# Differential attention scores: two products over 128 rows per map, or three over 64 rows with the two maps one above the other in the array

## The chip, the cores and the metric

The kernel runs on one core of one Trainium2 chip. The metric is the device time of one execution in microseconds (us); 729.48 us is the median of three runs of the kernel before (729.27, 729.48 and 730.88).

## The reference, cut to what matters

The program is a two-layer sequence model for 512 tokens of width 1024: a Mamba-2 layer (projections, a causal convolution, a chunked state-space scan, an out projection), then a layer of differential attention with eight heads, then a last RMS norm. All is float32. The change concerns the scores of the attention:

```python
DIFF_HEADS, DIFF_HEAD_DIM = 8, 64
k = kv[..., :1024].reshape(b, s, DIFF_HEADS, 2, DIFF_HEAD_DIM)      # two key maps per head
q = qg[..., :1024].reshape(b, nblk, 128, DIFF_HEADS, 2, DIFF_HEAD_DIM)
...
scores = einsum("bhiqd,bhikd->bhiqk", qb, k) / sqrt(64)             # i: the two maps
scores = scores - slopes[h] * dist
probs = softmax(where(key chunk <= query chunk, scores, -inf))
weights = probs[:, :, 0] - lam * probs[:, :, 1]
out = einsum("bhqk,bhke->bqhe", weights, v)
```

Each head thus has two score maps, and each is a product over only 64 features.

## The kernel before, in words

**Precision.** Nearly every product is made of three. An operand is kept as a rounded high part of type float32r and a low part (the value less its high part, rounded to float32r too); high by high, high by low and low by high are summed in PSUM, low by low is left out. `mm3` issues these three for the projections. TensorE works through one float32r product in one pass.

**The two streams on TensorE.** In the second half of the program, from about 440 us on, one stream `stream_b` yields the dense products in the order of `ORDER_B`: projections `pv` (values), `pk`, `pq`, `pt` (keys, queries and gates, two of them out of one weight tile, in `feat_proj`) and `pb` and `pc` (the output projection). A loop over the eight heads h and the four query blocks t of 128 rows draws on it: `scores(h, t)`, a third of a share of dense work, the transposes of the block before (`turn`), the rest of the share, the products with the values of the block before (`values`). The dense work is there to cover what DVE and ACT do between the two steps of a block. `T.on` makes TensorE issue in just the order in which the code is written; DVE and ACT are reordered by the scheduler in this part, by its own model, except at the very end.

**Keys and queries.** `feat_proj` leaves the 128 features of one head (64 of map 0, then 64 of map 1) on the 128 partitions of a PSUM bank `pf` (`pk` and `pq` in the profile), all 512 tokens wide. Lines 750 to 758 take it apart by map m. For keys, slot m of the tile `k2` gets the map's high half in its own 64 partitions and its low half in the other 64: one ACT copy and one DVE subtraction of 64 x 512 for each map. For queries, slot m of `q2` gets the high half in both places (two ACT copies for each map), and the tile `q_lo` gets the low half in the map's own partitions; the other 64 partitions of `q_lo` are zero, set once by four memsets on GpSimd (line 897). All ACT and DVE rows of this have the line 55 of a helper; they go by their tiles `k`, `q` and `q_lo`.

**Scores.** `scores(h, t)` works on n = 128 (t + 1) keys. For each map it takes a PSUM bank `sc` and issues two products over all 128 partitions: `q2` by `k2` (high by high from the one half of the partitions, high by low from the other) and `q_lo` by `k2` (low by high, and zero by the rest). DVE then adds the distance penalty and takes the row maximum out of the bank (`s<-sc,bias` in the profile), ACT makes the exponential. There are 32 such visits with four products each, that is, 16 products of each of the widths 128, 256, 384 and 512 in each of the two kinds.

**PSUM.** `ss_bank` hands out banks in turn: three buffers under the tag `ss`, and each fourth one in this part from the four `mm` buffers of the dense stream.

**A product of half width in the first half.** `ssd` makes the scan's products `pyd` from 64 stationary columns each, for the two halves of the output partitions (line 615, `for r in (slice(0, 64), slice(64, 128))`): 16 such products for each bank, issued alternately for the one and the other half. They are of plain float32, which the trace shows as two records per product.

Of the kernel before, what the change touches and what calls it, by code (L numbers as in the profile page):

```python
# [9 lines left out]
F32 = mybir.dt.float32  # L10
F32R = mybir.dt.float32r
I32 = mybir.dt.int32
AF = mybir.ActivationFunctionType
ALU = mybir.AluOpType
# [3 lines left out]
P = 128  # L18
S = 512
# [44 lines left out]
def trunk(ctx, tc, x, x_t, par, w_dt, w_in, w_out, w_kvqg, w_bo, d_skip, lam_qk, fin_g, out):  # L64
    nc = tc.nc
    V, A, T = (Ordered(tc, e) for e in (nc.vector, nc.scalar, nc.tensor))
    GP = nc.gpsimd
# [7 lines left out]
    def mm_bank(name):  # L75
        return psum.tile([P, 512], F32, tag="mm", name=name, bufs=4)
# [4 lines left out]
    def ss_bank(name):  # L81
        turns[0] += 1
        tag = "mm" if turns[0] % turns[1] >= 3 else "ss"
        return psum.tile([P, 512], F32, tag=tag, name=name, bufs=3 if tag == "ss" else 4)

    def long_bank(name):
        return psum.tile([P, 512], F32, tag="long", name=name)
# [118 lines left out]
    def use_b(seg, first=None, pace=None):  # L206
        i = segs.index(seg)
        while pieces:
            lay(pieces.pop(0))
        if i + 2 < len(segs) and fetched[0] == i + 2:  # L210
            loaded[i + 2] = load(i + 2)
        if seg == ("o", 3, 0):
            for piece in loaded.pop(i + 2)():
                lay(piece)
        if i + 1 in loaded:
            new = loaded.pop(i + 1)()
            pace = pace or 32 // len(new)
            pieces.extend(p + (pace if k else first or pace,) for k, p in enumerate(new))
        return ready.pop(seg)
# [15 lines left out]
    def mm3(ps, lhs, rhs, first, last, **kw):  # L235
        (lh, ll), (rh, rl) = lhs, rhs
        T.matmul(ps, lhsT=lh, rhs=rh, start=first, stop=False, **kw)
        T.matmul(ps, lhsT=lh, rhs=rl, start=False, stop=False, **kw)
        T.matmul(ps, lhsT=ll, rhs=rh, start=False, stop=last, **kw)
# [191 lines left out]
    q2 = sm.tile([P, P], F32, name="q2")  # L431
# [281 lines left out]
    cp = ctx.enter_context(tc.tile_pool(name="cp", bufs=1))  # L713
# [12 lines left out]
                yield 1  # L726
            A.copy(v_sb[:, t, cs], pv[:, 0:256])

    q_lo = [cp.tile([P, 2, S], F32R, name=f"q_lo{i}") for i in range(2)]
    kT, qT, gT, oT = {}, {}, {}, {}  # L730

    def feat_proj(pair):
        wh, wl = use_b((pair[0], pair, 0))
        for i in range(2):
            kind, h = pair[2 * i], int(pair[2 * i + 1])
            pf = mm_bank(f"p{kind}{h}")
            cs = slice(i * P, (i + 1) * P)
            for k in range(KD):
                mm3(pf, (wh[:, k, cs], wl[:, k, cs]), (hh[:, k, :], hl[:, k, :]), k == 0, k == KD - 1)
                yield 2  # L740
            if kind == "t":

                th = small.tile([P, S], F32, tag="wide", name=f"th{h}", bufs=2)
                A.activation(th, pf, AF.Tanh, scale=0.5)
                gt = cp2.tile([P, S], F32, tag="gt", name=f"gt{h}", bufs=3)
                V.scalar_tensor_tensor(out=gt, in0=th, scalar=1.0, in1=pf, op0=ALU.add, op1=ALU.mult)
                gT[h] = gt
            else:

                two = cp2.tile([P, 2, S], F32R, tag=f"{kind}2", name=f"{kind}2_{h}", bufs=4 if kind == "k" else 2)  # L750
                for m in range(2):
                    own, far = slice(64 * m, 64 * m + 64), slice(64 - 64 * m, 128 - 64 * m)
                    A.copy(two[own, m, :], pf[own, :])
                    if kind == "q":
                        A.copy(two[far, m, :], pf[own, :])
                    V.tensor_tensor(out=two[far, m, :] if kind == "k" else q_lo[h % 2][own, m, :], in0=pf[own, :],
                                    in1=two[own, m, :].bitcast(F32), op=ALU.subtract)
                (kT if kind == "k" else qT)[h] = two
            done.add(f"{kind}{h}")

# [17 lines left out]
    def stream_b():  # L778
        for it in ORDER_B:
            if it[0] == "c":  # L780
                yield from rows()
                return
            yield from b_out(int(it[1])) if it[0] == "b" else v_proj(int(it[1])) if it[0] == "v" else feat_proj(it)
            done.add(it)
# [3 lines left out]
    def scores(h, t):  # L788

        if t == 0:  # L790
            bias = cp2.tile([P, S], F32, tag="bias", name=f"bias{h}")
            V.tensor_scalar(out=bias, in0=dist, scalar1=-(2.0 ** (2 - h)), scalar2=None, op0=ALU.mult)
            st[h] = (bias, small.tile([P, 2, NT], F32, tag="mx", name=f"mx{h}"),
                     small.tile([P, 2, NT], F32, tag="sums", name=f"sums{h}"), [],
                     small.tile([P, NT], F32, tag="ratio", name=f"ratio{h}"), long_bank(f"po{h}"), [],
                     cp2.tile([P, NT, P], F32, tag="on", name=f"on{h}", bufs=2),
                     small.tile([P, NT], F32, tag="o_ss", name=f"o_ss{h}"))
        bias, mx, sums, s = st[h][0:4]
        k2, q2, ql = kT[h], qT[h], q_lo[h % 2]
        n = (t + 1) * P  # L800
        tq = slice(t * P, (t + 1) * P)
        s.append([cp2.tile([P, S], F32, tag=f"s{i}", name=f"s{h}_{t}_{i}", bufs=2) for i in range(2)])
        for i in range(2):
            ps = ss_bank(f"sc{h}_{t}_{i}")
            T.matmul(ps[:, :n], lhsT=q2[:, i, tq], rhs=k2[:, i, :n], start=True, stop=False)
            T.matmul(ps[:, :n], lhsT=ql[:, i, tq], rhs=k2[:, i, :n], start=False, stop=True)
            so = s[t][i][:, :n]
            V.tensor_tensor_reduce(out=so, in0=ps[:, :n], in1=bias[:, S - n:], scale=-0.125, scalar=3e38,
                                   op0=ALU.add, op1=ALU.min, accum_out=mx[:, i, t:t + 1])
            A.activation(so, so, AF.Exp, scale=-1.0, bias=mx[:, i, t:t + 1], accum_out=sums[:, i, t:t + 1])  # L810
# [81 lines left out]
    V.tensor_copy(dist, disti)  # L892
    A.activation(dist, dist, AF.Abs)
    GP.memset(dist[0:64, S - 64:S], BIG)
    for i in range(2):
        for m in range(2):
            GP.memset(q_lo[i][64 - 64 * m:128 - 64 * m, m, :].bitcast(F32), 0.0)
    lq = cp2.tile([P, 4, 64], F32, tag="gt", name="lq", bufs=3)
    nc.sync.dma_start(lq.rearrange("p a d -> p (a d)"), lam_qk.rearrange("a d -> (a d)").partition_broadcast(P))
    lqv = lq.rearrange("p (a b) d -> p a b d", b=2)  # L900
# [38 lines left out]
    def half(t, n):  # L939
        hs = slice(n * 512, (n + 1) * 512)  # L940
        return x_tok[:, t, hs], fg[:, hs], ot[t][:, hs], out[t * P:(t + 1) * P, hs]
# [40 lines left out]
    for h in range(DH):  # L982
        for t in range(NT):
            share = (13.0, 15.3, 17.6, 19.35)[t]
            if (h, t) == (DH - 1, 2):
                break
            scores(h, t)
            beside(share / 3)
            if h > 1 and t == 0:
                gate_head(h - 2)  # L990
            if last:
                turn(*last)
            beside(share * 2 / 3)
            if last:
                values(*last)
                if t == 0:
                    norm_head(h - 1)
            last = h, t


    h = DH - 1
    turns[:] = [0, 1]
    fg = res.tile([P, D], F32, tag="hT_lo", name="fg")
    nc.sync.dma_start(fg[:], fin_g.partition_broadcast(P))
    scores(h, 2)
    beside(6)
    gate_head(h - 1)
# [3 lines left out]
    norm_head(h, 0, 2)  # L1011
    beside(7.6)
    scores(h, 3)
    ot += [cp2.tile([P, D], F32, tag="k2", name=f"ot{t}", bufs=4) for t in range(NT)]
    beside(2)
# [45 lines left out]
    y, f, o, dst = half(3, 0)  # L1061
# [71 lines left out]
```

## Time and profile before

| What | Value |
|---|---|
| Median of three runs | 729.48 us (729.27 to 730.88) |
| The profiled execution: time, span | 729.15 us, 727.0 us |
| TensorE (PE) busy | 713.5 us, 98% of the span |
| TensorE weight loads (PEld) busy | 593.1 us, 82% |
| VectorE (DVE) busy | 528.0 us, 73% |
| ScalarE (ACT) busy | 433.7 us, 60% |
| GpSimd (POOL) busy | 117.7 us, 16% |
| HBM traffic | 97 GB/s over the span |
| Chain that ended last, share by engine | PE 90%, DVE 7%, ACT 1%, issue 1% |

A row of the trace's timeline gives the start in us, the time in us, the engine, the line, the operation, the tiles written and read, for TensorE the part of the array that is used (rows by columns), the shape, and how many instructions in a row are merged. TensorE's products are pipelined: the recorded time of one contains its way through the array, so a run of equal products starts one every 0.23 us though each is recorded with 0.40 us. What a product costs TensorE is the distance from its start to that of the next (its pitch). The busy time of PE is a union of such records and hides gaps that are shorter than the overlap. "PEld" rows are the loads of the stationary operand, which run beside the products.

### The profile page before, as it was taken

The page shows a single profiled execution, that of the slowest core. Times are in us where ns is not written, and L with a number is a line of the kernel's source. Part 1 is how long each engine was busy: PE and PEld are TensorE (multiplying, and loading weights), DVE is VectorE, ACT ScalarE, POOL GpSimd, SP SyncE. Part 2 cuts the span into 40 slices and gives each one's busy share as a digit, 9 for nine tenths or more (in the row PEclk, how much of TensorE's full clock was granted, in tenths as well). Part 3 has the DMA queues.
Part 4 walks back from the last instruction along what each step waited for, and adds up shares of the span by engine and source line. Part 5 has one row for each costly group of instructions (what it writes and reads, how often), then busy time and mean ns, then how long its engine had stood idle before and what let it go on. Part 6 is the DMA issues. An engine that isn't in the chain of part 4 may idle for free.

```text
span 727.0 us, 10819 instructions
## 1 busy us (share of the span) xinstructions
PE 713.5 (98%) x3989; PEld 593.1 (82%) x3989; DVE 528.0 (73%) x1202; ACT 433.7 (60%) x965; POOL 117.7 (16%) x158
## 2 busy tenths in 40 slices
PE   9999999999999999999999999999999999999996
PEld 7787888888888888887788869888988898889874
DVE  4688964979479668569995846657667857785886
ACT  5948573654735527527534348667766756756566
POOL 0108241412315024150110101000000000000002
PEclk9999999999999999999999999999999999999999
DMA  8634313314133231231122310331221131122003
GB/s 302 233 131 162 116 59 117 117 58 175 58 117 116 95 137 60 91 142 59 59 70 105 116 59 9 117 115 59 94 82 58 59 117 59 59 90 85 29 1 115
DMA packets 12916, 70.86 MB, mean 97 GB/s; under 512 B 1728, under 2 KB 2496, under 8 KB 5312
## 3 DMA queue, kind: packets, MB, share of 16 engines
q1 hardware_dynamic: 12576, 69.90, 26.5%
q8 instruction: 31, 0.51, 0.3%
q10 hardware_dynamic: 288, 0.28, 0.1%
q14 instruction: 21, 0.17, 0.1%
HBM read 68.02 MB, written 2.16 MB: 97 GB/s over the span
## 4 chain that ended last, share of the span: by engine, by line
PE 90%; DVE 7%; ACT 1%; issue 1%; POOL 0%; ACTq 0%; DVEq 0%; POOLq 0%
PE pg L55 21%; PE po L55 14%; PE pz L55 12%; PE pt L55 7%; PE pv L55 6%; PE pq L55 6%; PE pk L55 6%; PE pb L55 3%; PE sc L55 3%; PE pyd L55 2%; PE pc L55 2%; DVE wlo L55 2%; DVE xc L55 2%; PE pyt L55 1%; PE pxt L55 1%; PE psA L55 1%
## 5 line engine op out<-in xcount | busy, mean ns | idle before, releaser
L55 DVE SCALAR_TENSOR_TENSOR wlo<-raw,prm,whi 128x512 fp32r<-128x512 f32 (+1 forms) x256 | 150.4, 633 | 52.7 <-ACT whi L55 51.3
L55 ACT ACTIVATE whi<-raw,prm 128x512 fp32r<-128x512 f32 (+1 forms) x256 | 136.8, 606 | 81.4 <-PE pg L55 30.1
L55 PE MATMUL pg<-a_hi,whi 128*128 128x512 f32 x256 | 103.3, 404 | 1.5 <-DVE y_c L55 1.5
L55 PE MATMUL pg<-a_hi,wlo 128*128 128x512 f32 x256 | 102.3, 402 | 0.0
L55 PE MATMUL pg<-a_lo,whi 128*128 128x512 f32 x256 | 102.3, 400 | 0.0
L55 DVE SCALAR_TENSOR_TENSOR xc<-pg,prc,xc 128x511 f32<-128x511 f32 (+2 forms) x96 | 69.6, 738 | 4.8 <-ACT xc L55 4.4
L55 PEld LDWEIGHTS pg<-a_hi,whi 128*128 128x128 f32 x256 | 48.1, 188 | 13.1 <-issue 1.9
L55 PEld LDWEIGHTS pg<-a_hi,wlo 128*128 128x128 f32 x256 | 48.1, 188 | 11.0
L55 PEld LDWEIGHTS pg<-a_lo,whi 128*128 128x128 f32 x256 | 48.1, 188 | 10.7
L55 PE MATMUL po<-whi,yh 128*128 128x512 f32 x128 | 51.4, 402 | 1.5 <-DVE xc L55 0.8
L55 PE MATMUL po<-wlo,yh 128*128 128x512 f32 x128 | 51.1, 399 | 0.0
L55 PE MATMUL po<-whi,yl 128*128 128x512 f32 x128 | 50.4, 398 | 0.0
L55 PE MATMUL pz<-wlo,a_hi 128*128 128x512 f32 x128 | 50.3, 399 | 0.0
L55 PE MATMUL pz<-whi,a_lo 128*128 128x512 f32 x128 | 49.8, 398 | 0.0
L55 PE MATMUL pz<-whi,a_hi 128*128 128x512 f32 x128 | 49.6, 401 | 0.0
L971 POOL TENSOR_TENSOR ot<-ot,fg 128x512 f32<-128x512 f32 x4 | 5.1, 1289 | 256.9 <-ACT ot L55 256.9
L55 ACT ACTIVATE s<-s,mx 128x128 f32<-128x128 f32 (+3 forms) x64 | 35.5, 556 | 9.6 <-DVE mx L55 9.1
L55 ACT ACTIVATE xc<-pg,prc 128x512 f32<-128x512 f32 x32 | 24.6, 773 | 26.6 <-DVE pg L55 26.5
L589 POOL TENSOR_TENSOR xe<-xdt,tok 128x256 f32<-128x256 f32 x24 | 17.3, 749 | 139.6 <-DVE xdt L55 139.6
L55 DVE CUSTOM_DVE_ANT_0 s<-sc,bias 128x128 f32<-128x128 f32 (+3 forms) x64 | 29.4, 488 | 12.2 <-PE sc L55 11.7
L55 ACT ACTIVATE xc<-xc 128x512 f32<-128x512 f32 x32 | 20.0, 629 | 28.3 <-DVE xc L55 28.2
L55 PE MATMUL pv<-whi,b_hi 128*128 128x256 f32 x128 | 36.6, 286 | 0.0
(243 smaller groups left out, 1719.7 us busy)
## 6 DMA issues: line engine op xcount, KB each, us to landing
raw<-in_w_in SPq DMA_DIRECT2D x23, 1024.0 KB, 4.8
raw<-in_w_kvqg SPq DMA_DIRECT2D x16, 1024.0 KB, 4.8
dec<-acs_d SPq DMA_DIRECT2D x8, 1024.0 KB, 4.8
raw<-in_w_out SPq DMA_DIRECT2D x8, 1024.0 KB, 4.8
raw<-in_w_bo SPq DMA_DIRECT2D x4, 1024.0 KB, 4.8
x_tok<-in_x SPq DMA_DIRECT2D x4, 512.0 KB, 9.3
out<-ot SPq DMA_DIRECT2D x7, 256.0 KB, 2.4
raw<-in_w_in SPq DMA_DIRECT2D x4, 256.0 KB, 5.8
```

Source lines behind the costliest of these rows:

```text
L55: i = op(*args, **kw)
L589: GP.tensor_tensor(out=xe[:, c], in0=xdt[:, c], in1=toe_tok[:, c, hs].unsqueeze(2).to_broadcast([P, R, HD]), op=ALU.mult)
L971: GP.tensor_tensor(out=o, in0=o, in1=f, op=ALU.mult)
```

## The change: what it does, and the diff

Keys and queries of a head are each kept as one tile with a high slot and a low slot of 128 x 512, both maps one above the other as they leave the projection: one ACT copy and one DVE subtraction for each. The tile `q_lo` and its memsets go. In `scores` both banks are taken first, and then six products follow: high by high, high by low, low by high, each for map 0 from partitions 0 to 63 and for map 1 from partitions 64 to 127, the maps alternating. In the built program these six are addressed to parts of 64 rows by 128 columns of the array, the one at row 0 and the other at row 64, where before each product had all 128 rows. DVE and ACT read the two banks as before.

```diff
-    q_lo = [cp.tile([P, 2, S], F32R, name=f"q_lo{i}") for i in range(2)]
...
                 two = cp2.tile([P, 2, S], F32R, tag=f"{kind}2", name=f"{kind}2_{h}", bufs=4 if kind == "k" else 2)
-                for m in range(2):
-                    own, far = slice(64 * m, 64 * m + 64), slice(64 - 64 * m, 128 - 64 * m)
-                    A.copy(two[own, m, :], pf[own, :])
-                    if kind == "q":
-                        A.copy(two[far, m, :], pf[own, :])
-                    V.tensor_tensor(out=two[far, m, :] if kind == "k" else q_lo[h % 2][own, m, :], in0=pf[own, :],
-                                    in1=two[own, m, :].bitcast(F32), op=ALU.subtract)
+                A.copy(two[:, 0, :], pf)
+                V.tensor_tensor(out=two[:, 1, :], in0=pf, in1=two[:, 0, :].bitcast(F32), op=ALU.subtract)
...
-        k2, q2, ql = kT[h], qT[h], q_lo[h % 2]
+        k2, q2 = kT[h], qT[h]
...
+        pss = [ss_bank(f"sc{h}_{t}_{i}") for i in range(2)]
+        for qp, kp in ((0, 0), (0, 1), (1, 0)):
+            for i in range(2):
+                own = slice(64 * i, 64 * i + 64)
+                T.matmul(pss[i][:, :n], lhsT=q2[own, qp, tq], rhs=k2[own, kp, :n], start=qp + kp == 0, stop=qp == 1)
         for i in range(2):
-            ps = ss_bank(f"sc{h}_{t}_{i}")
-            T.matmul(ps[:, :n], lhsT=q2[:, i, tq], rhs=k2[:, i, :n], start=True, stop=False)
-            T.matmul(ps[:, :n], lhsT=ql[:, i, tq], rhs=k2[:, i, :n], start=False, stop=True)
+            ps = pss[i]
             so = s[t][i][:, :n]
...
-    for i in range(2):
-        for m in range(2):
-            GP.memset(q_lo[i][64 - 64 * m:128 - 64 * m, m, :].bitcast(F32), 0.0)
```

The next two pieces are TensorE's order around the scores of the first head's last block, before and then with the change. A number behind an underscore is a block, a map or a buffer: `sc_3_0` is the bank of block 3, map 0; `po` is the bank of the product with the values, `pk` that of a key projection.

```order
L55 MATMUL po_4322<-v_sb,wT_1_4467 128x128 x2
L55 MATMUL sc_3_0_4497<-k_0_4185,q_0_4265 128x512
L55 MATMUL sc_3_0_4497<-k_0_4185,q_lo_3959 128x512
L55 MATMUL sc_3_1_4502<-k_0_4185,q_0_4265 128x512
L55 MATMUL sc_3_1_4502<-k_0_4185,q_lo_3959 128x512
L55 MATMUL pk_4512<-b_hi,whi_4311 128x512
```

```order
L55 MATMUL po_4308<-v_sb,wT_1_4455 128x128 x2
L55 MATMUL sc_3_0_4485<-k_0_4179,q_0_4255 128x512
L55 MATMUL sc_3_1_4486<-k_0_4179,q_0_4255 128x512
L55 MATMUL sc_3_0_4485<-k_0_4179,q_0_4255 128x512
L55 MATMUL sc_3_1_4486<-k_0_4179,q_0_4255 128x512
L55 MATMUL sc_3_0_4485<-k_0_4179,q_0_4255 128x512
L55 MATMUL sc_3_1_4486<-k_0_4179,q_0_4255 128x512
L55 MATMUL pk_4500<-b_hi,whi_4297 128x512
```

Four products, map by map, have become six, with the maps alternating; the neighbours on both sides still use all 128 rows, and nothing else moves on TensorE in the whole program beside these 32 places.

The next two pieces are ACT's order around the queries of the third head (`q_2`), before and with the change; `pq` is the bank of the query projection.

```order
L55 COPY wT_3_4614<-pt_3_4609 128x512
L55 CAST q_2_4632<-pq_4563 64x512 x2
L55 COPY on_4323<-po_4322 128x128
L55 ACTIVATE sq_3_4648,o_ss_4324<-on_4323 128x128
L55 CAST q_2_4632<-pq_4563 64x512 x2
L55 ACTIVATE s_1_0_4666,sums_4581<-s_1_0_4666,mx_4580 128x256
```

```order
L55 COPY wT_3_4602<-pt_3_4597 128x512
L55 CAST q_2_4620<-pq_4549 128x512
L55 COPY on_4309<-po_4308 128x128
L55 ACTIVATE sq_3_4632,o_ss_4310<-on_4309 128x128
L55 ACTIVATE s_1_0_4650,sums_4567<-s_1_0_4650,mx_4566 128x256
```

Four copies of half height have become one of full height; the rest stands as it stood.

## The prediction

> **What bounds the kernel now.** I read the page first, then the busy time by stretches of the second half, where the change lies, then who waits for whom there. From the page:
>
> ```profile
> span 727.0 us, 10819 instructions
> PE 713.5 (98%) x3989; PEld 593.1 (82%) x3989; DVE 528.0 (73%) x1202; ACT 433.7 (60%) x965; POOL 117.7 (16%) x158
> ```
>
> The stretches (start and end in us, then each engine's busy time and instructions), and TensorE's waits from 430 us to the end:
>
> ```profile
> core 0: us, PE busy (x) PEld busy (x) DVE busy (x) ACT busy (x) POOL busy (x), PEclk, DMA share, GB/s
> 480.00:560.00 80.00, 80.00 (x446) 68.86 (x445) 56.72 (x174) 55.53 (x160) 0.00 (x0) 1.00 0.22 79
> 640.00:700.00 60.00, 60.00 (x359) 52.86 (x358) 45.21 (x133) 34.45 (x99) 0.00 (x0) 1.00 0.18 62
> ...
> PE pc L55 <- DVE pc L55: 0.5, 1, 0.5
> PE pc L55 <- DVE ol L55: 0.4, 1, 0.4
> ```
>
> TensorE has no idle time from 480 to 700 us, and in the whole second half it waits for another engine for 0.9 us, both times in the output projection `pc` at the very end. So a microsecond more or less of TensorE's work in a score visit is a microsecond of the kernel, and work taken from DVE and ACT is worth nothing until TensorE waits for them. What a product costs TensorE is its pitch, which the timeline shows for each width of the scores (one pair of neighbours each):
>
> ```profile
> 506.44 0.27 PE L55 MATMUL sc<-k,q_lo 128*128 128x128 f32 x1
> 506.55 0.27 PE L55 MATMUL sc<-k,q 128*128 128x128 f32 x1
> ...
> 513.16 0.28 PE L55 MATMUL sc<-k,q_lo 128*128 128x256 f32 x1
> 513.28 0.28 PE L55 MATMUL sc<-k,q 128*128 128x256 f32 x1
> ...
> 548.28 0.34 PE L55 MATMUL sc<-k,q_lo 128*128 128x384 f32 x1
> 548.46 0.34 PE L55 MATMUL sc<-k,q 128*128 128x384 f32 x1
> ...
> 555.98 0.39 PE L55 MATMUL sc<-k,q_lo 128*128 128x512 f32 x1
> 556.21 0.40 PE L55 MATMUL sc<-k,q 128*128 128x512 f32 x1
> ...
> L55 PE MATMUL sc<-k,q 128*128 128x512 f32 x16 | 6.9, 430 | 0.0
> ```
>
> The pitches are 0.11, 0.12, 0.18 and 0.23 us, together 0.64. Each width comes in 8 visits of four products (the last row: 16 of one kind, as many of the other), so the scores hold TensorE for 4 x 8 x 0.64 = 20.5 us. That is all that the change can shorten.
>
> **The products, if two halves of the array work at once.** Six products of 64 rows then take the time of three: one pitch of each visit goes, 8 x 0.64 = -5.1 us. If the two of a pair go one after the other, six pitches stand for four: +10.2 us. The trace has no product of 64 rows. Its nearest rows are `pyd`, products of 64 columns, alternately on one and the other half of the array's columns:
>
> ```profile
> 77.29 0.59 PE L55 MATMUL psA<-xe,bt 128*128 128x256 f32 x2
> 77.72 0.59 PE L55 MATMUL psB<-xe,bt 128*128 128x256 f32 x2
> 78.24 1.15 PE L55 MATMUL pyd<-xdt,dec 128*64 128x64 f32 x32
> 79.33 0.50 PE L55 MATMUL pg<-a_hi,whi 128*128 128x512 f32 x1
> 79.66 0.40 PE L55 MATMUL pg<-a_lo,whi 128*128 128x512 f32 x1
> ...
> 78.24 1.01 PEld L55 LDWEIGHTS pyd<-xdt,dec 128*64 128x64 f32 x32 [0.33 <-PE psA L55]
> 79.32 0.19 PEld L55 LDWEIGHTS pg<-a_hi,whi 128*128 128x128 f32 x1
> 79.43 0.19 PEld L55 LDWEIGHTS pg<-a_lo,whi 128*128 128x128 f32 x1
> ...
> L55 PEld LDWEIGHTS pyd<-xdt,dec x512: 132/138/138, 78.2 to 408.3; 128*64 128x64 f32 x171
> ```
>
> Two float32 records of 256 take 0.43 us (`psA` to `psB`), so one of 64 should take 0.43 / 2 / 4 = 0.054 us, and 32 of them 1.72 us. The 32 loads span 1.01 us with the last one's 0.14 in it: the last begins 0.87 us after the first, 15 steps for 16 pairs, 0.058 us a pair. The two halves do run at once, loads and products both. I take this for the halves of rows too, as the nearest row: -5.1 us.
>
> **The way into and out of a visit.** The same rows show what it costs to leave the full array and come back. From `psB` at 77.72 to the second `pg` at 79.66 are 1.94 us. The work itself is 0.43 (`psB`) + 16 x 0.058 = 0.93 (`pyd`) + 0.23 (the first `pg`, by the pitch of 512 columns above) = 1.59. The remaining 0.35 us is the switch. It can be placed: `pyd` should start at 77.72 + 0.43 = 78.15 and starts 0.09 later; its first load runs beside nothing; `pg` comes 0.10 late; and the first `pg` takes 0.33 to the next instead of 0.23, since its load, too, begins only when all is done (79.32, with the product). An ordinary product has its load under the one before it.
>
> With 64 rows and 128 columns the load at the entry is longer. Two loads of 128 columns follow at 0.11 us (79.32 and 79.43), so one of 64 columns is about half of that, and the longer one adds some 0.05: 0.40 us a visit. At width 128, where the load and not the product sets the pitch (0.11 against 0.06, half of the pitch of 256 columns), the load that now stands free at entry and exit was already paid in the pitch: 0.05 less at either end, 0.30. Over 32 visits that is 24 x 0.40 + 8 x 0.30 = +12.0 us. The bounds are 0 (row halves need no switch) and, above, 0.45 a visit at all widths, 14.4 us; I take 12.0, since no row shows a part of the array changed without this cost.
>
> The Trainium skill speaks to this in "TensorEngine Tiling (Array Packing)", section Key Properties: changing the tiling mode, not only the tile, drains TensorE. The late start after `psB` and the late `pg` agree with it. By that rule the sum is the one below; the same skill's "TensorE: Matmul & The Clock Gate", section Part 3: Packing small matmuls, has row halves start within some 4 ns of each other and names no price for the switch, and by that alone the sum would be the gain of the first rival.
>
> **Keys, queries and the memsets.** By kinds of instruction in the second half:
>
> ```profile
> L55 ACT CAST q<-pq 64x512 fp32r<-64x512 f32 x32 | 18.6, 581 | 10.4 <-PE pq L55 6.4 <-DVE q_lo L55 3.8
> L55 ACT CAST k<-pk 64x512 fp32r<-64x512 f32 x16 | 9.3, 579 | 7.4 <-PE pk L55 3.7 <-DVE k L55 3.6
> L55 DVE TENSOR_TENSOR q_lo<-pq,q 64x512 fp32r<-64x512 f32 x16 | 11.0, 689 | 13.3 <-ACT q L55 13.2
> L55 DVE TENSOR_TENSOR k<-pk,k 64x512 fp32r<-64x512 f32 x16 | 11.0, 689 | 5.4 <-ACT k L55 5.1
> ...
> L55 ACT CAST b_hi<-btp 128x512 fp32r<-128x512 f32 x6 | 3.2, 586 | 1.8 <-PE btp L55 1.8
> L55 DVE TENSOR_TENSOR b_lo<-btp,b_hi 128x512 fp32r<-128x512 f32 x8 | 5.1, 682 | 2.9 <-ACT b_hi L55 2.9
> ```
>
> A full-height copy out of PSUM (0.59 us, `b_hi`) costs ACT what a half-height one costs, and so does the subtraction on DVE (0.68, `b_lo`). ACT goes from 48 copies to 16, 27.9 to 9.4 us; DVE from 32 subtractions to 16, 22.0 to 10.9. Both gains lie beside a TensorE that waits for neither: 0. Were that cover gone, what could be won back is the 0.9 us of waits above, and those are not for keys or queries. The memsets are on GpSimd, which is not busy at all in the two stretches above: 0.
>
> **Banks and the tail.** Both banks are now taken before the first product, so the second must be free two pitches sooner. DVE empties a visit's banks within 2 us (702.51 + 0.69 below, against the visit's 701.25), and visits lie 6 us apart (506 to 513 above): no wait. But map 0 is now ready with the fifth product and not with the second. Behind it stands DVE's reduction, then ACT's exponential. In the steady part they have 5 us; in the last visit TensorE waits for what is queued behind them:
>
> ```profile
> 701.25 0.39 PE L55 MATMUL sc<-k,q 128*128 128x512 f32 x1
> 701.90 0.69 DVE L55 CUSTOM_DVE_ANT_0 s<-sc,bias 128x512 f32<-128x512 f32 x1
> 702.51 0.69 DVE L55 CUSTOM_DVE_ANT_0 s<-sc,bias 128x512 f32<-128x512 f32 x1
> ...
> 703.35 0.71 ACT L55 ACTIVATE s<-s,mx 128x512 f32<-128x512 f32 x1
> 704.19 0.16 DVE L55 RECIPROCAL ratio<-sums 128x1 f32<-128x1 f32 x1 [0.44 <-ACT s L55]
> 705.15 0.41 DVE L55 TENSOR_TENSOR ol<-pot,oh 128x256 fp32r<-128x256 f32 x1
> 705.62 0.50 PE L55 MATMUL pc<-whi,ol 128*128 128x512 f32 x1 [0.42 <-DVE ol L55]
> ```
>
> DVE begins 0.65 us after the visit does. With the change the fifth product starts after 0.09 (drain) + 0.11 (load) + 2 x 0.23 = 0.66 and is recorded with 0.40: DVE begins at about 1.1, that is 0.45 later. TensorE's own visit grows from 0.92 to 3 x 0.23 + 0.40 = 1.09, by 0.17, so the wait before `pc` grows by the difference, +0.3 us.
>
> **Sum.** -5.1 + 12.0 + 0 + 0.3 = +7.2 us. The profiled execution took 729.15 us (span 727.0 and 2.15 around it), so 736.35; the median of the runs shown is 729.48, 0.33 above it, and the same shift gives **736.7 us**. With 0.35 to 0.45 a visit it is 734 to 739.
>
> **The rivals.**
>
> *Row halves change without a switch.* Then -5.1 remains, and in the last visit map 0 is ready at 2 x 0.23 + 0.40 = 0.86 instead of 0.65, so that the wait before `pc` takes that visit's gain back and a little more, some +0.5: -4.6, 724.9 us, faster. For it: rows, unlike columns, could be two full-width loads in one mode, and no row of this trace excludes it. Against it: the only switch that the trace shows costs 0.35 us every time. It decides below 5.1 / 32 = 0.16 us a visit.
>
> *A switch at about that price.* Half a drain and the loads hidden, 0.12 to 0.2 us: 728 to 731, no change that can be told.
>
> *The loads of the two halves go one after the other.* Each carries 128 columns, twice those of `pyd`, and two at 0.11 make a pair at least 0.22. A visit's three pairs are then 0.66 at the three smaller widths and 0.70 at 512, 2.68 against 2.56 us a head: +1.0, with the switch at 0.40 everywhere (12.8) and the tail +14.1: 743.6 us.
>
> *The pair does not overlap.* +10.2, alone 739.7 us; with the switch 751.7. Against it is `pyd`; for it, that nothing here has two row halves.
>
> **How the numbers follow.** Forecast 0.52; no switch 0.22; a switch at break-even 0.06; serial loads 0.08; no overlap with the switch 0.07, without 0.05. The range 724 to 744 leaves out only the slow end and the edge of the fast rival. A measurement tells some 0.2% (1.5 us) from no change: faster 0.22 + 0.02 = 0.24, same 0.04, slower 0.72.
>
> **What would show it.** Right: the `sc` records come in pairs a few ns apart, pairs at 0.11, 0.12, 0.18 and 0.23 us, the first `sc` load starts 0.09 late with nothing beside it, and the first dense product behind a visit takes 0.33 us. Copies and subtractions have 16 rows of 128x512 each, and TensorE still waits only in `pc`, longer before `ol`. Wrong: no gap at the entry and a hidden first load (724), pairs at 0.22 (744), or `sc` starts spaced one full pitch apart (740 to 752).

## The result, and the profile after

The change makes the kernel slower: 738.51 us (median of four runs, 738.17 to 740.24) against 729.94 us for the kernel before on the same chip (four runs, 729.27 to 730.88), a ratio of 1.0125 with a 95% interval of 1.0111 to 1.0139. The forecast was 736.7 us. In a second comparison, beside the experiments below, it was 738.14 against 731.11, 1.0093 (1.0066 to 1.0121). The page of the changed kernel begins:

```profile
span 738.5 us, 10880 instructions
PE 721.2 (98%) x4053; PEld 589.8 (80%) x4053; DVE 520.8 (71%) x1186; ACT 415.3 (56%) x933; POOL 116.2 (16%) x154
```

DVE and ACT have become lighter and TensorE longer. Here is a visit of the changed kernel for a last block (512 keys), first TensorE's products and then its weight loads in the timeline:

```profile
561.80 0.61 PE L55 MATMUL po<-v_sb,wT 128*128 128x128 f32 x4
562.34 0.96 PE L55 MATMUL sc<-k,q 64*128 64x512 f32 x6
563.23 0.50 PE L55 MATMUL pk<-b_hi,whi 128*128 128x512 f32 x1
563.57 0.39 PE L55 MATMUL pk<-b_lo,whi 128*128 128x512 f32 x1
563.80 0.40 PE L55 MATMUL pk<-b_hi,wlo 128*128 128x512 f32 x1
...
562.34 0.53 PEld L55 LDWEIGHTS sc<-k,q 64*128 64x128 f32 x6
563.23 0.19 PEld L55 LDWEIGHTS pk<-b_hi,whi 128*128 128x128 f32 x1 [0.36 <-issue]
563.34 0.19 PEld L55 LDWEIGHTS pk<-b_lo,whi 128*128 128x128 f32 x1
```

Six products of 512 columns are through in 0.96 us, where six one after the other would have at least 5 x 0.23 and the record of the last one, 0.39, some 1.5: the halves of the array do work at once. In the records the two products of a first pair start 3 to 4 ns apart, in every visit. But the first load of the visit begins with the first product (562.34) and not under the one before, the way back again has a load that stands free (563.23, in both lists), and the first `pk` takes 0.34 us to the next where 0.23 is its pitch. From the start of the last product ahead of a visit to the start of the second behind it, less the own pitches of these two neighbours, a visit costs, as means over the 8 visits of each width and summed:

| Keys in the visit | 128 | 256 | 384 | 512 | all 32 visits |
|---|---|---|---|---|---|
| Before, us | 0.45 | 0.48 | 0.70 | 0.92 | 20.4 |
| The change, us | 0.68 | 0.75 | 0.92 | 1.10 | 27.6 |
| Three quarters of before (three pitches) | 0.34 | 0.36 | 0.53 | 0.69 | 15.3 |
| Rest: the switch | 0.34 | 0.39 | 0.39 | 0.40 | 12.2 |

The visits alone are +7.1 us. To leave out the first 480 us, where TensorE's work is the same, I count from the first score product to the end of the span: 727.0 - 478.8 = 248.2 us before, and 255.7 with the change (738.5 - 482.7, taken before rounding), +7.5.

Keys and queries, by kinds of instruction:

```profile
L55 ACT CAST q<-pq 128x512 fp32r<-128x512 f32 x8 | 4.7, 587 | 8.7 <-PE pq L55 8.7
L55 ACT CAST k<-pk 128x512 fp32r<-128x512 f32 x8 | 4.6, 576 | 4.4 <-PE pk L55 4.4
...
L55 DVE TENSOR_TENSOR k<-pk,k 128x512 fp32r<-128x512 f32 x8 | 5.5, 690 | 4.5 <-ACT k L55 4.5
L55 DVE TENSOR_TENSOR q<-pq,q 128x512 fp32r<-128x512 f32 x8 | 5.5, 690 | 7.0 <-ACT q L55 7.0
```

ACT's share fell from 27.9 to 9.3 us and DVE's from 22.0 to 11.0.

The last visit and the wait behind it, in the timeline:

```profile
712.36 0.97 PE L55 MATMUL sc<-k,q 64*128 64x512 f32 x6
713.26 0.50 PE L55 MATMUL pc<-whi,oh 128*128 128x512 f32 x1
713.36 0.69 DVE L55 CUSTOM_DVE_ANT_0 s<-sc,bias 128x512 f32<-128x512 f32 x1 [0.50 <-PE sc L55]
...
713.60 0.40 PE L55 MATMUL pc<-wlo,oh 128*128 128x512 f32 x1
...
714.73 0.55 PE L55 MATMUL pt<-ident,s 128*128 128x128 f32 x3 [0.17 <-DVE mx L55]
...
716.62 0.41 DVE L55 TENSOR_TENSOR ol<-pot,oh 128x256 fp32r<-128x256 f32 x1
...
717.09 0.50 PE L55 MATMUL pc<-whi,ol 128*128 128x512 f32 x1 [0.43 <-DVE ol L55]
```

The kernel before, at the same place:

```profile
702.38 0.39 PE L55 MATMUL pc<-wlo,oh 128*128 128x512 f32 x1
...
703.27 0.55 PE L55 MATMUL pt<-ident,s 128*128 128x128 f32 x3
...
705.62 0.50 PE L55 MATMUL pc<-whi,ol 128*128 128x512 f32 x1 [0.42 <-DVE ol L55]
```

DVE begins 1.00 us after the visit does, 0.65 before. The cost of a visit in the table reaches to the start of the second product behind it, here the second `pc`. From there to the `pc` that waits for `ol` are 3.49 us (713.60 to 717.09); before they were 3.24 (702.38 to 705.62). That is +0.25 that the visits do not hold. Nearly all of it has come by the transposes `pt`, which start 1.13 us behind the second `pc` instead of 0.89, with a new wait of 0.17 for DVE's reduction (`mx`). The wait for `ol` itself is as long as before.

### The profile page after: what moved, and what is told of

The parts are those of the page before. It is cut to its first block, busy times and chain, and to the rows that moved or that the text cites. A ratio compares the mean times of both kernels' runs of the same rounds, so it can differ in the third digit from the quotient of the medians.

```text
span 738.5 us, 10880 instructions
## 1 busy us (share of the span) xinstructions
PE 721.2 (98%) x4053; PEld 589.8 (80%) x4053; DVE 520.8 (71%) x1186; ACT 415.3 (56%) x933; POOL 116.2 (16%) x154
## 4 chain that ended last, share of the span: by engine, by line
PE 81%; DVE 11%; ACT 4%; DMA 2%; issue 1%; SPq 0%; POOL 0%; ACTq 0%; DVEq 0%
PE pg L55 18%; PE po L55 13%; PE pz L55 9%; PE pt L55 7%; PE pv L55 6%; PE pq L55 6%; PE pk L55 6%; PE pb L55 3%; DVE wlo L55 3%; PE sc L55 3%; DVE xc L55 2%; PE pyd L55 2%; PE pc L55 2%; ACT whi L55 1%; DMA raw<-in_w_in 1%
## 5 line engine op out<-in xcount | busy, mean ns | idle before, releaser
L55 DVE SCALAR_TENSOR_TENSOR wlo<-raw,prm,whi 128x512 fp32r<-128x512 f32 (+1 forms) x256 | 154.8, 652 | 58.6 <-ACT whi L55 57.5
L55 ACT ACTIVATE s<-s,mx 128x128 f32<-128x128 f32 (+3 forms) x64 | 35.5, 556 | 15.3 <-DVE mx L55 15.0
L553 POOL TENSOR_TENSOR dec<-dec,tok 128x512 f32<-128x512 f32 x32 | 37.2, 1192 | 0.6
```

The costliest lines, as they stand in the source:

```text
L55: i = op(*args, **kw)
L553: GP.tensor_tensor(out=dec[:, h], in0=dec[:, h], in1=acs_tok[:, :, R * g + h].unsqueeze(2).to_broadcast([P, NQ, P]), op=ALU.subtract)
```

## The experiments

The theory: TensorE pays a fixed price each time it goes from the full array to halves of 64 rows and back, whatever is done in between, and that price alone makes the loss. The rivals: products of half height are themselves slow; or the new layout and the order that it brings on DVE and ACT cost something.

**The layout without the halves.** The scores are four products over all 128 rows again:

```diff
-        for qp, kp in ((0, 0), (0, 1), (1, 0)):
-            for i in range(2):
-                own = slice(64 * i, 64 * i + 64)
-                T.matmul(pss[i][:, :n], lhsT=q2[own, qp, tq], rhs=k2[own, kp, :n], start=qp + kp == 0, stop=qp == 1)
+        for i in range(2):
+            T.matmul(pss[i][:, :n], lhsT=q2[:, 0, tq], rhs=k2[:, i, :n], start=True, stop=False)
+            T.matmul(pss[i][:, :n], lhsT=q2[:, 1, tq], rhs=k2[:, i, :n], start=False, stop=True)
```

> Keys and queries are laid out as in the change (one copy and one subtraction each, no memsets), but the scores are again four products over all 128 rows for a visit, in the order of before, on tiles that no longer hold what such products need: each sums over both maps, so the scores are other numbers. Theory (all of the loss is the switch between the full array and its halves, and DVE and ACT hide the cheaper layout): within 0.7 us of the kernel before, 729.5 to 730.5, visits of 20.4 us in all. Rival (the layout, its tiles' places or the new order on DVE and ACT cost the part of +8.6 that the visits do not hold, some 1.4 us): 731 to 732. Second rival (the lighter ACT and DVE bring something): 727 to 729.

Measured: 730.14 us against 731.11, ratio 0.9994 (0.9974 to 1.0014), no difference. Its span, and the first and last start of its score products:

```profile
span 728.4 us, 10752 instructions
...
L55 PE MATMUL sc<-k,q x128: 223/336/481, 480.2 to 703.4; 128*128 128x128 f32 x32, 128*128 128x256 f32 x32, 128*128 128x384 f32 x32, 128*128 128x512 f32 x32
```

From the first score product to the end are 728.4 - 480.2 = 248.2 us, as before to the tenth, and the visits are 20.4 us. So the layout costs nothing, and 18.6 us less on ACT and 11.0 less on DVE bring nothing. The whole loss is in how the products are made.

**The maps one after the other.** The two loops are exchanged, so that the three products of map 0 stand ahead of the three of map 1:

```diff
-        for qp, kp in ((0, 0), (0, 1), (1, 0)):
-            for i in range(2):
-                own = slice(64 * i, 64 * i + 64)
+        for i in range(2):
+            own = slice(64 * i, 64 * i + 64)
+            for qp, kp in ((0, 0), (0, 1), (1, 0)):
```

> The six products of a visit in another order: three for map 0 on rows 0 to 63, then three for map 1 on rows 64 to 127. Theory (only two products on different halves run at once): only the third of map 0 can run beside the first of map 1, so a visit has five pitches and the switch in place of three: 16 x 0.64 = +10.2 us over the change, 748.7 us; if the two do not overlap either, six pitches, 753.8. Rival (row halves need no neighbour to be quick, the time of a visit is loads and drains): as the change, 738 to 740.

Measured: 740.58 us (two runs), against 731.11. Neither 748.7 nor 753.8 came: my theory missed here, and the rival's number was nearer, though not for the rival's reason. A visit of this kernel, and which of its products are under way at 561.20 us:

```profile
561.07 0.97 PE L55 MATMUL sc<-k,q 64*128 64x512 f32 x6
561.96 0.50 PE L55 MATMUL pk<-b_hi,whi 128*128 128x512 f32 x1
...
561.07 0.50 PE L55 MATMUL sc<-k,q 64*128 64x512 f32 x2
```

Six are again through in 0.97 us, and 0.13 us into the visit two are under way, both within the first 0.50 us. The first three in the program are all of map 0, so the second one under way is the fourth: it starts about 10 ns after the first, ahead of the second and third, and so in all 32 visits. The signals in the records agree: the two products that tell DVE of a finished map, the third and the sixth of the program, stand last in time, fifth and sixth. Visits total 27.8 us against 27.6. TensorE had undone the edit, and the run did not say what the overlap is worth. From the first score product on it took 738.4 - 481.4 = 257.0 us, 1.3 more than the change: 0.2 in the visits, the rest at the end, where TensorE now waits 1.8 us for ACT's `oh`.

**All on one half.** This run replaces it:

```diff
-                own = slice(64 * i, 64 * i + 64)
+                own = slice(0, 64)
```

> The change with all six products of a visit on rows 0 to 63: map 1 is computed from map 0's queries and keys, so half of the scores are other numbers. The order with the maps apart still ran its pairs side by side, so it did not tell what the overlap is worth; this does. Theory (products overlap only on different halves): six pitches a visit instead of three, 3 x 8 x 0.64 = +15.3 us over the change, 42.8 us of visits in all, 753.5 us. Rival (a product of 64 rows is quick whatever stands beside it): visits of 27.6 us and the change's time, 738 us.

Measured: 754.57 us (two runs) against 730.25, and 42.7 us of visits, both as the theory had it. A visit of 512 keys, and what is under way 0.13 us into it:

```profile
500.93 1.65 PE L55 MATMUL sc<-k,q 64*128 64x512 f32 x6
502.51 0.50 PE L55 MATMUL pk<-b_hi,whi 128*128 128x512 f32 x1
...
500.93 0.49 PE L55 MATMUL sc<-k,q 64*128 64x512 f32 x1
```

One is under way, not two, and six take 1.65 us. A product of 64 rows has the same pitch as one of 128. The overlap saves three pitches of six, 42.7 - 27.6 = 15.1 us, of which the change had spent 10.2 by making six products out of four. The rest of 5 us is its whole gain. The switch is there without any overlap: 42.7 us less six pitches a visit (2 x 15.3) leaves 12.1, against 12.2 with the change.

**Fewer visits.** Blocks 0 and 1, and 2 and 3, are scored together:

```diff
-            scores(h, t)
+            if t % 2 == 0:
+                scores(h, t)
+                scores(h, t + 1)
...
-        s.append([cp2.tile([P, S], F32, tag=f"s{i}", name=f"s{h}_{t}_{i}", bufs=2) for i in range(2)])
+        s.append([cp2.tile([P, S], F32, tag=f"s{i}", name=f"s{h}_{t}_{i}", bufs=3) for i in range(2)])
```

> The change, with the scores of blocks 0 and 1, and of 2 and 3, issued right behind each other (one more buffer for each score tile), except for the last two blocks of the last head: 17 visits instead of 32, with the same products. Theory (the loss is a switch of 0.34 to 0.40 us a visit, whatever the visit holds): 15 switches fewer, -5.7 us against the change, some 732.5 us. Rival (the loss is in the products of half height themselves): as the change, 738. Second rival (TensorE now waits for the four banks or for DVE and ACT behind a longer visit): between the two or above, with waits of TensorE at the scores or the transposes.

Measured: 733.93 us against 730.70, ratio 1.0041 (1.0021 to 1.0060). A visit with 128 and 256 keys:

```profile
566.97 0.95 PE L55 MATMUL sc<-k,q 64*128 64x128 f32 x12
567.85 0.50 PE L55 MATMUL pq<-b_hi,whi 128*128 128x512 f32 x1
```

The visits are 22.0 us in all, 5.5 less than with 32, or 0.37 for each of the 15 switches that went, and from the first score product on it takes 731.2 - 481.3 = 249.9 us, 5.8 less than the change. No wait for the four banks shows. It is still 1.7 us longer than before: 17 switches cost more than the products save.

**More visits.** One step of the dense stream between the first pair and the two others:

```diff
         for qp, kp in ((0, 0), (0, 1), (1, 0)):
+            if kp and h < DH - 1:
+                due[0] -= next(dense[0])
```

> The change, with one step of the dense stream (three products over the full array, which would come later otherwise) put between the first pair and the other two pairs of every visit of the first seven heads: 28 visits more, with the same products. Theory (a switch of 0.34 to 0.40 us a visit): 28 x 0.38 = +10.7 us over the change, 749 us. Rival (the loss is in the products): as the change, 738 to 739.

Measured: 747.81 us (two runs) against 730.70; from the first score product on 745.9 - 479.6 = 266.3 us, 10.5 more than the change. The 60 visits are 38.2 us, so the 28 that were added cost 10.6 in all, 0.38 each. The price hangs on the number of switches and not on what lies between, in both directions.

**How far the order can be undone.** Two blocks a visit, with all six products of map 0 ahead of all six of map 1:

> Two blocks a visit as before, but all six products of map 0 ahead of all six of map 1. Theory (each half of the array takes its own products in order, and TensorE looks far enough ahead to start map 1's first product beside map 0's first): visits as with two blocks and alternating maps, 22.0 us in all, some 734 us. Rival (it looks only a few instructions ahead, three products and their loads at most): map 0's first products run alone, at least 8 x 0.3 us and up to 15 us more, 736 to 749 us.

Measured: 739.59 us (two runs) against 730.25. A visit with 128 and 256 keys:

```profile
568.12 1.23 PE L55 MATMUL sc<-k,q 64*128 64x128 f32 x12
569.28 0.50 PE L55 MATMUL pq<-b_hi,whi 128*128 128x512 f32 x1
```

Twelve take 1.23 us where alternating maps took 0.95, and the visits are 27.5 us in all. From the first score product on it takes 258.2 us, 8.2 more than with alternating maps: 5.5 in the visits, the rest at the end (the last section has the place). In the records the seventh product, map 1's first, starts with the third and not with the first, in the visits of 384 and 512 keys as in those of 128 and 256. So TensorE does take products for the other half out of turn, but from some four products ahead at most; the rival that it looks only a few instructions ahead holds.

**The kernel before and the change, once more.**

> The change itself, once more, beside the kernel before. Theory: +7.5 us (the visits +7.15, the wait near the end +0.35) and whatever of the 3.8 us that its first profile lost ahead of the scores was that execution's own, so 737.0 to 738.5 and a first score visit at 479 to 480 us. Rival (the change slows the part ahead of the scores as well, where its code is the same): the first score visit again at 482 us or later.

> The kernel before, unchanged, for a second profile of it. Theory (what lies ahead of the scores wanders from execution to execution): a first score visit anywhere from 478 to 482 us. Rival (that part is fixed for each kernel): 478.8 us again within 0.3.

Measured: the change 738.14 us against 731.11, its first score product at 480.8 us and 255.7 us from there to the end of its span of 736.5; the kernel before, 729.62 us, 479.2 and 248.3. What lies behind the first score product repeats to 0.1 us (255.7 both times, 248.2 and 248.3), and what lies ahead of it differs from one profile to the next: 478.8 and 479.2 before, 482.7 and 480.8 with the change, 479.6 to 481.4 in the other six. Of the 3.9 us that the first profile of the change lost ahead of the scores, 1.9 did not come back; 480.8 is later than the theory had it and earlier than the rival had.

No version with half products came out ahead of the kernel before. With 0.38 us a switch and 5.1 us to gain, halves pay from 13 visits or fewer, and two blocks a visit, which four PSUM banks allow, leave 16 at least with whole heads. Packing narrow blocks of two heads into shared banks might give 12 visits, worth some 0.5 us by the same estimate, less than a measurement here tells; it was not tried.

## Why the prediction was right

**The bound** was right: TensorE has no idle time in the scores, and only TensorE's work moved the time. The layout alone, with 48 fewer operations on ACT and DVE, gave 0.0 us.

**The overlap, -5.1 us,** was right, though the only rows for it were half columns. Half rows run at once at the full pitch, and the loads with them: from the second pair of a visit to the third are 0.11, 0.12, 0.17 and 0.23 us at the four widths, and a pair of width 128 thus takes one load of 0.11 us, not two. With that the rivals of serial loads and of no overlap are out; the run on one half shows what the latter would have been.

**The switch, +12.0 us,** was right: 12.2 measured, 0.34 us at width 128 (0.30 forecast) and 0.39 to 0.40 at the others (0.40 forecast). It has the parts that `pyd` showed for half columns. At the three larger widths a visit starts 0.09 us late, its first pair takes 0.10 more than a pitch (the free load), the first dense product behind it comes 0.09 late and takes 0.10 more than its pitch (the free load there). At width 128 the forecast took 0.05 off at either end; only the entry shows it. The Trainium skill ("TensorEngine Tiling (Array Packing)", section Key Properties) states that a change of the tiling mode drains TensorE; the two late starts of 0.09 us agree with it. The price came from the `pyd` rows. The fast rival, which decides below 0.16 us a visit, is out.

**The tail, +0.3 us,** came out at 0.25. Its cause was the one that was forecast, since DVE begins 1.00 us after a first product that is itself 0.09 late, the 1.1 of the prediction. Its place was not: the prediction had a longer wait before `ol` and no new wait of TensorE, but nearly all of it came one product group earlier, at the transposes.

**The sum, +7.2,** is +7.5 from the first score product on in both profiles: 7.1 in the visits, 0.25 behind the last one, and the remaining 0.1 in hundredths between the visits. (The prediction's narrower bounds are a slip: 0.35 to 0.45 us a visit give 735 to 739 and not 734 to 739.) The medians say +8.6 in the first comparison and +7.0 in the second. The profiles differ only ahead of the scores. One place of that can be read. In the first profile of the change TensorE waits 1.9 us there for a bank that DVE empties late. First DVE and GpSimd of that profile, then of the kernel before, at the same place in the program:

```profile
226.18 0.74 DVE L55 SCALAR_TENSOR_TENSOR wlo<-raw,prm,whi 128x512 fp32r<-128x512 f32 x1
227.17 1.53 DVE L55 SCALAR_TENSOR_TENSOR wlo<-raw,prm,whi 128x512 fp32r<-128x512 f32 x1
229.82 2.99 DVE L55 SCALAR_TENSOR_TENSOR wlo<-raw,prm,whi 128x512 fp32r<-128x512 f32 x2
...
226.69 0.27 POOL L551 COPY dec<-dec 128x8 f32<-128x8 f32 x1 [0.72 <-DMA dec<-acs_d]
227.04 5.22 POOL L553 TENSOR_TENSOR dec<-dec,tok 128x512 f32<-128x512 f32 x4
...
235.86 0.50 PE L55 MATMUL po<-whi,yh 128*128 128x512 f32 x1 [1.85 <-DVE x_tok L55]
```

```profile
224.78 0.74 DVE L55 SCALAR_TENSOR_TENSOR wlo<-raw,prm,whi 128x512 fp32r<-128x512 f32 x1
...
226.77 1.40 DVE L55 SCALAR_TENSOR_TENSOR wlo<-raw,prm,whi 128x512 fp32r<-128x512 f32 x2
...
227.20 0.36 POOL L551 COPY dec<-dec 128x8 f32<-128x8 f32 x1 [2.63 <-DMA dec<-acs_d]
227.65 4.47 POOL L553 TENSOR_TENSOR dec<-dec,tok 128x512 f32<-128x512 f32 x4
```

GpSimd waits there for a transfer. In the profile of the change it had it at 226.69 us, with three of DVE's splits (`wlo`) still to come; its four operations ran beside them, and a split took 1.5 us instead of 0.7. In the kernel before the transfer came 0.5 us later (227.20) and DVE stood 1.4 us earlier (224.78 at the first split against 226.18), so that DVE was nearly through. The second profile of the change has the same wait of TensorE with 1.1 us. The layout alone has it (1.9 us) with no change in its scores, the maps one after the other and two blocks a visit have it (1.8 and 1.1), and the other three kernels with half products do not. So the half products do not make it. The two profiles of the kernel before do not have it either; whether the new layout favours it is not shown, and the ten runs of the layout alone tell no difference in time. That the order of the two decides is read from the traces and was not tried by itself, and whether the rest of the wandering (1.1 us at 69 us in the first profile of the change, 0.4 at 334) has the same cause stays open.

## What to carry to other kernels

Here halves of the array doubled the rate of products with 64 rows, but TensorE lost time at both borders; count visits, not products: a visit paid 0.38 us to save one pitch of 0.11 to 0.23 us. Before a product is cut to fit a half, see whether the idle half of a full product can be given useful work, as the kernel before did for three quarters of its rows, since then the cut has less to win. A price found in the trace for a neighbouring kind of operation (half columns) carried over to the new one (half rows) within a few hundredths of a microsecond.

## What the runs showed of the hardware that was not expected

TensorE does not keep to the program's order between its halves. With three products of one half ahead of three of the other, the fourth started 10 ns after the first, and two were under way at once; with six ahead, the seventh started with the third. Within a half the widths and the signals of the products came in the program's order.

After a wait of TensorE near the end the granted clock was lower in one run and not in another. In the run with two blocks and the maps apart, its stages from 716 to 720 us, behind a wait of 1.82 us for ACT's `oh`, read (granted clock in the third column from the right):

```profile
714.97 0.49 PE L55 MATMUL pc<-whi,oh 128*128 128x512 f32 x1 [1.82 <-ACT oh L55]
...
716.00:718.00 2.00, 2.00 (x10) 1.92 (x9) 1.35 (x2) 0.77 (x3) 0.00 (x0) 0.62 0.00 0
718.00:720.00 2.00, 2.00 (x6) 1.52 (x6) 0.77 (x2) 1.46 (x7) 0.00 (x0) 0.53 0.00 0
```

The granted clock was 0.62 and 0.53 there and products stood 0.43 us apart instead of 0.23. With the maps one after the other, a wait of 1.8 us at the same place was followed by a granted clock of 1.00, so the wait alone does not decide it, and what does stays open.
